# Three edits around TensorE's longest waits: a scan in four pieces, the last block's squares summed by matmul, the last output group channel by channel

## The chip, the cores and the metric

The kernel runs on one core of one Trainium2 chip. The metric is the device time of one execution in microseconds; lower is better. Engines are named as the profile names them: PE (TensorE matmul; PEld its weight loads), DVE (VectorE), ACT (ScalarE), POOL (GpSimd), SP (SyncE, which issues most DMAs). All data are 32-bit floating point. A matmul of type fp32r takes one pass; one of plain fp32 shows as two passes in the profile.

## The reference

One encoder layer on 2048 prompt tokens and, with the same weights, on 256 sample tokens (2304 in all), model width 1024:

```python
def encoder_layer(x, ...):
    h = rmsnorm(x, norm1_w)
    p = h @ w_in
    mq, mk, mv, mo, gates, aq, ak, av = jnp.split(p, cuts, axis=-1)
    m_out = mlstm_mixer(mq, mk, mv, mo, gates, b_gates, mh_norm_w)   # both directions, 8 heads of 64
    a_out = attention_mixer(aq, ak, av, q_norm_w, k_norm_w)          # 8 query heads, 2 key heads, rotary
    x = x + jnp.concatenate([m_out, a_out], axis=-1) @ w_out
    h = rmsnorm(x, norm2_w)
    u = centred_dwconv(h @ w_up, conv_w, conv_b)                     # width 3
    a, g = jnp.split(u, 2, axis=-1)
    return x + (jax.nn.silu(g) * a) @ w_down                         # inner width 2816
y = rmsnorm(encoder_layer(x, ...), final_norm_w)
# rmsnorm(x, w): x * rsqrt(mean(x * x) + 1e-6) * w
# mLSTM, per step: m_new = max(logf + m, i)  (the running maximum that stabilises the gates, forward and backward)
```

## The kernel before, in words

Tokens lie along the free axis in most stages (channels on the 128 partitions), in 18 tiles of 128 tokens. Products at full precision are made of three fp32r products each, of high and low halves (`split`, `split_w`: ACT rounds the high half, DVE subtracts to get the low half). The stages, in order of time:

- `phase_a` (0 to about 180 us): per tile the attention projections and gate pre-activations, `post1` (rotary) and `post2`; after each four tiles `gates(i0, n)` computes log-sigmoids and, tile by tile, PE transposes them and ACT (L307) copies them into `g.rows` (40 partitions, 2 rows, 2304 tokens): row 0 the input gate, row 1 the forget gate; partitions 0 to 7 are the forward heads, 32 to 39 the backward heads.
- `gate_math` (about 180 to 235 us): for both sequences (`SEGS`) a forward scan along tokens (L363) and a backward scan (L365) on DVE, state = max(state + logf, i). PE then transposes the scanned rows (L401, tiles `gpt`) for the exponents of the mLSTM.
- Attention and mLSTM, interleaved, with the output projection (`phase_c`, L983) in their later part (to about 1830 us). PE's mLSTM projections (L711, tiles `mj`; L721, tiles `mv`) share one PSUM buffer, which ACT empties (L717, L724, L727). `phase_c` takes blocks of 256 tokens in `ORDER`, the last of them block 7: four groups `z` of two channels; `post` adds the residual (L990), squares on ACT (L993) and sums on DVE into `acc` (L995); `tail` folds `acc` (L998), calls `rstd_bc` and scales (L1002). The last block's `tail` is `c_end`, called when the first two column groups of the feed-forward have begun.
- `phase_d`: `up_phase` (to about 2817 us; products L1140, a one-level Strassen-like scheme with seven products; input splits L1064 and L1065, weight splits L1112 and L1113, weight sums L1098), then `down_phase` (products L1399), three blocks of 768 tokens in two halves, each half's output in two groups of four channels. `add` adds a PSUM bank to the accumulator (L1387) and at the last product of a half calls `square`: ACT squares (L1353), POOL adds the squares up (L1357) except in the very last group (`end`), where each square is kept by itself, and ACT scales by the final norm's weight (L1358). `finish` calls `rstd_bc`, multiplies (L1365) and stores (L1366).

`rstd_bc` gives 1/sqrt(mean of squares + EPS), on all partitions: per 128 tokens PE multiplies each square tile with a column of ones (L128), DVE adds EPS (L131), then POOL raises to -1/2 (L142) or, with `act`, ACT takes the root (L135) and DVE inverts it and refines it once (L136 to L140); PE broadcasts the result to all partitions (L144).

What sets the order: the tile framework writes each engine's instruction sequence at build time from a planned timeline (`schedule_with_timeline_sim=True`), with priorities that follow the program's order; `tc.high_priority(offset=...)` moves some ahead (the splits of the feed-forward's late inputs among them). On the chip each engine works its sequence in that order, and semaphores hold an instruction until its inputs are there.

Of the kernel before, what the change touches and what calls it, by code (L numbers as in the profile page):

```python
# [119 lines left out]
def rstd_bc(g, sp, pp, sqs, n, ptag, name, bufs=1, act=False):  # L120


    nc = g.nc
    k = n // P
    ps = pp.tile([P, 512], F32, tag=ptag, name="rs_" + name, bufs=bufs)
    for t in range(k):
        for i, sq in enumerate(sqs):
            nc.tensor.matmul(ps[:, 504 + 2 * t:506 + 2 * t], sq[:, t * P:(t + 1) * P], g.ones, start=i == 0,  # L128
                             stop=i == len(sqs) - 1)
    r = sp.tile([P, 4], F32, tag="rcol", name="rcol_" + name)[:, 0:k]  # L130
    nc.vector.tensor_scalar(r, ps[:, 504:504 + 2 * k].rearrange("p (t o) -> p t o", o=2)[:, :, 0], EPS, None, ALU.add)  # L131
    if act:
        v = r
        r, u = (sp.tile([P, 4], F32, tag=f"rcol{z}", name=f"rcol{z}_" + name, bufs=1)[:, 0:k] for z in range(2))
        nc.scalar.activation(r, v, AF.Sqrt)  # L135
        nc.vector.reciprocal(r, r)  # L136
        nc.vector.tensor_tensor(u, r, r, ALU.mult)
        nc.vector.tensor_tensor(u, u, v, ALU.mult)
        nc.vector.tensor_scalar(u, u, -0.5, 1.5, ALU.mult, ALU.add)
        nc.vector.tensor_tensor(r, r, u, ALU.mult)  # L140
    else:
        nc.gpsimd.tensor_tensor(r, r, g.mhalf[:, 0:k], ALU.pow)  # L142
    for t in range(k):
        nc.tensor.matmul(ps[:, t * P:(t + 1) * P], r[:, t:t + 1].to_broadcast([P, P]), g.ident, start=True, stop=True)  # L144
    return ps[:, 0:n]


def phase_a(g, tc, sw, st_x, after_x, after_mm, after_pj):
# [3 lines left out]
    with ExitStack() as st:  # L152
# [132 lines left out]
        def gates(i0, n):  # L285

            f = g.gtm[:, i0:i0 + n, 1, :]
            t4 = sp.tile([P, 4, 4, 16], F32, tag="t4", name=f"t4_{i0}", bufs=1)
            na, u, ln, dl = (t4[:, k, 0:n] for k in range(4))
            nc.vector.scalar_tensor_tensor(na, f, -1.0, f, ALU.mult, ALU.min)  # L290
            nc.scalar.activation(na, na, AF.Exp)
            nc.vector.tensor_scalar(u, na, 1.0, None, ALU.add)
            nc.vector.scalar_tensor_tensor(dl, u, 1.0, na, ALU.subtract, ALU.subtract)
            nc.scalar.activation(ln, u, AF.Ln)
            nc.scalar.activation(g.lnr[:, i0:i0 + n], g.rt[:, i0:i0 + n], AF.Ln)
            nc.vector.tensor_scalar(u, u, -0.5, 1.5, ALU.mult, ALU.add)
            nc.vector.tensor_tensor(dl, dl, u, ALU.mult)
            nc.vector.tensor_tensor(ln, ln, dl, ALU.subtract)
            nc.vector.scalar_tensor_tensor(f, f, 0.0, ln, ALU.min, ALU.subtract)
            for i in range(i0, i0 + n):  # L300
                gp = gps[i % 3]
                nc.vector.tensor_copy(gp.rearrange("p a (b z) -> p a b z", b=2)[:, :, :, 0:8],
                                      g.gtm[:, i].rearrange("p a (b h) -> p a b h", b=2))
                pg = pp.tile([40, 2, P], F32, tag="pk", name=f"pg{i}")
                for a in range(2):
                    nc.tensor.transpose(pg[:, a, :], gp[:, a, 0:40], g.ident)
                nc.scalar.activation(g.rows[:, :, i * P:(i + 1) * P], pg, AF.Copy)  # L307

        def post2(i, kz):
            pk = pp.tile([P, 2, P], F32R, tag="pk", name=f"pk{i}")  # L310
# [45 lines left out]
def gate_math(g, tc):  # L356
# [3 lines left out]
    m = frow  # L360
    for (c0, c1) in SEGS:
        s = slice(c0 * P, c1 * P)
        nc.vector.tensor_tensor_scan(m[0:8, s], frow[0:8, s], irow[0:8, s], 0.0, ALU.add, ALU.max)  # L363
        r = slice(c1 * P - 1, c0 * P - 1 if c0 else None, -1)
        nc.vector.tensor_tensor_scan(m[32:40, r], frow[32:40, r], irow[32:40, r], 0.0, ALU.add, ALU.max)  # L365
    with ExitStack() as st:
# [572 lines left out]
def phase_c(g, sn, sp, pp, wps):  # L939
# [49 lines left out]
    def post(b, z, x, po, acc):  # L989
        nc.vector.tensor_tensor(x[z], po, x[z], ALU.add)  # L990
        g.st.dma_start(g.x1_d[b, :, 2 * z:2 * z + 2], x[z])
        q = acc if z == 0 else sp.tile([P, 2, BT], F32, tag="sq", name=f"csq{b}_{z}", bufs=1)
        nc.scalar.activation(q, x[z], AF.Square, scale=1.0 / 32.0)  # L993
        if z:
            nc.vector.tensor_tensor(acc, acc, q, ALU.add)  # L995

    def tail(b, x, acc):
        nc.vector.tensor_tensor(acc[:, 0], acc[:, 0], acc[:, 1], ALU.add)  # L998
        r = rstd_bc(g, sp, pp, [acc[:, 0]], BT, "r", f"c{b}", act=b == ORDER[-1])
        for z in range(4):  # L1000
            for o in range(2):
                nc.vector.scalar_tensor_tensor(x[z][:, o], x[z][:, o], g.n2w[:, 2 * z + o:2 * z + o + 1],  # L1002
                                               r, ALU.mult, ALU.mult)
            (nc.gpsimd if b == ORDER[-1] else g.st).dma_start(g.n2_d[:, 2 * z:2 * z + 2, b * BT:(b + 1) * BT], x[z])
        g.normed.add(b)
# [309 lines left out]
def down_phase(g, tc, st, s1, sl, banks):  # L1315
# [33 lines left out]
    def square(accs, b, c, z, sms, end):  # L1349
        a = accs[c][:, Z[z]]  # L1350
        first = not sms
        q = sp.tile([P, H], F32, tag=f"sm{z}" if first else "sq", name=f"sq{b}_{c}_{z}", bufs=1 if first else SQB)
        nc.scalar.activation(q, a, AF.Square, scale=1.0 / 32.0)  # L1353
        if first or end:
            sms.append(q)
        else:
            nc.gpsimd.tensor_tensor(sms[0], sms[0], q, ALU.add)  # L1357
        nc.scalar.activation(a, a, AF.Copy, scale=g.fw[:, c:c + 1])  # L1358

    def finish(accs, b, z, sms, bank):  # L1360
        r = rstd_bc(g, sp, bank, sms, H, "p", f"d{b}_{z}", bufs=4)

        def out(c):
            a = accs[c][:, Z[z]]
            nc.vector.tensor_tensor(a, a, r, ALU.mult)  # L1365
            g.st.dma_start(g.yT[c, :, b * BLK + z * H:b * BLK + (z + 1) * H], a)  # L1366
        for c in range(NCC):
            out(c)
# [3 lines left out]
    for b in range(ND):  # L1372
# [18 lines left out]
        def mul(ps, k, more):  # L1391
            for g0, g1 in ((0, 4), (4, 8), (8, NG)):
                t = act_tile(b, k, g0, g1)
                for z in range(g0, g1, 2):
                    for i, w in enumerate(wts(b, k, z, min(z + 2, g1))):
                        gi = z + i
                        for c in range(HALF):
                            for m, (aa, bb) in enumerate(((0, 0), (0, 1), (1, 0))):
                                nc.tensor.matmul(ps[c], w[:, aa, c, :], t[:, gi - g0, bb, 0:H],  # L1399
                                                 start=gi == 0 and m == 0 and not more,  # L1400
                                                 stop=gi == NG - 1 and m == 2, skip_group_check=more)
        p1 = newbanks(one, "f")
        mul(p1, "11", False)
        add(p1, 0, 0, False)
# [18 lines left out]
def body(tc, aps, phases="abcd"):  # L1423
# [5 lines left out]
    with ExitStack() as st:  # L1429
# [24 lines left out]
        nc.vector.tensor_copy(g.identr, g.ident)  # L1454
        g.mhalf = kp.tile([P, 16], F32, name="mhalf")
        nc.gpsimd.memset(g.mhalf, -0.5)
        g.ones = kp.tile([P, 2], F32, name="ones")
        nc.gpsimd.memset(g.ones, 1.0)
        nw = kp.tile([P, 3, NCC], F32, name="nw")
# [172 lines left out]
```

## Time and profile before

| | |
|---|---|
| median of 3 runs | 3344.66 us (3342.89 to 3348.4) |
| the profiled execution's own time | 3337.43 us |
| its span, first to last instruction | 3335.7 us |
| instructions | 53337 |
| PE busy | 3248.2 us |
| DVE, ACT, POOL busy | 2429.6, 2003.1, 512.4 us |
| mean granted TensorE clock | 0.988 |

How to read the profile's rows. A timeline row has start, duration, engine, source line, operation, output and input by name, shapes, count, and in brackets the idle time of that engine just before it with what ended it. Several instructions of one line in a row are merged into one row with their count. A row of waits reads "who waited <- for what: us in total, times, longest". A row of stretches has the stretch, its length, then busy time and instruction count of PE, PEld, DVE, ACT and POOL, the granted clock, the busy share of the DMA engines and GB/s. Names are cut to their stem: `rs_c` is the PSUM tile of `rstd_bc` for `phase_c`, `rs_d` that for `down_phase`; `rcol` their small columns; `cacc`, `csq` and `cx` the sums, squares and residuals of `phase_c`.

### The profile page before, as it was taken

How to read it: one execution, taken by the hardware profiler on the slowest of the kernel's cores; microseconds unless marked ns; L12 is line 12 of the kernel's file. 1: busy time of each engine (PE TensorE's matmuls, PEld its weight loads, DVE VectorE, ACT ScalarE, POOL GpSimd, SP SyncE). 2: the span in 40 equal slices, each digit the busy share in tenths (PEclk: the TensorE clock that was granted, in tenths of full speed). 3: DMA queues.
4: the chain of work that ended last, by engine and by line, in shares of the span. 5: the costliest groups of instructions: out<-in, count | busy, mean ns of one | idle time of the engine just before them, and what ended most of it. 6: DMA issues, size and time to landing. Idle time of an engine off the chain costs nothing.

```text
span 3335.7 us, 53337 instructions
## 1 busy us (share of the span) xinstructions
PE 3248.2 (97%) x19494; PEld 3025.2 (91%) x19494; DVE 2429.6 (73%) x3765; ACT 2003.1 (60%) x3769; POOL 512.4 (15%) x915
## 2 busy tenths in 40 slices
PE   8989999999999999999999899999999999999998
PEld 7878888888887878878889899999999999999998
DVE  7755676677657777776665999998888788656664
ACT  5646666666665676665552555666676667454543
POOL 4551033213232322300000000000000000020201
PEclk9999999999999999999999899999999999999999
DMA  9973333333335433533227666668576567967663
GB/s 354 315 202 108 112 113 102 110 110 92 109 113 176 128 113 116 169 97 106 85 88 269 227 237 213 232 231 274 204 262 240 193 211 243 321 222 274 223 237 112
DMA packets 364301, 612.31 MB, mean 184 GB/s; under 512 B 31605, under 2 KB 220455, under 8 KB 364039
## 3 DMA queue, kind: packets, MB, share of 16 engines
q1 hardware_dynamic: 330727, 563.14, 50.1%
q0 software_dynamic: 11856, 33.96, 3.7%
q10 hardware_dynamic: 21456, 11.80, 1.2%
q8 instruction: 154, 2.52, 0.3%
q14 instruction: 108, 0.88, 0.1%
HBM read 444.85 MB, written 163.93 MB: 183 GB/s over the span
## 4 chain that ended last, share of the span: by engine, by line
PE 77%; issue 6%; DMA 5%; DVE 5%; ACT 4%; POOL 2%; SPq 0%; POOLq 0%; ACTq 0%; DVEq 0%
PE pa L1140 17%; PE pc L1140 8%; PE pf L1399 5%; PE po L983 5%; PE pj L237 5%; PE pb L1140 4%; PE mj L711 4%; PE mv L721 3%; PE ps L576 3%; PE ps L577 3%; PE pv L593 3%; PE pv L595 3%; PE pv L594 3%; PE px L553 2%; PE ph L1399 2%
## 5 line engine op out<-in xcount | busy, mean ns | idle before, releaser
L582 DVE TENSOR_TENSOR xx<-pe,xx 128x1024 fp32r<-128x1024 f32 x260 | 319.1, 1228 | 127.3 <-ACT xx L581 125.8
L555 DVE TENSOR_REDUCE mx<-px 128x1 f32<-128x1024 f32 x256 | 311.0, 1218 | 101.3 <-PE px L553 100.1
L580 ACT ACTIVATE pe<-ps 128x1024 f32<-128x1024 f32 x260 | 266.3, 1024 | 172.5 <-PE ps L577 163.4
L581 ACT ACTIVATE xx<-pe 128x1024 fp32r<-128x1024 f32 x260 | 274.9, 1058 | 5.2 <-ACT pe L580 0.3
L1357 POOL TENSOR_TENSOR sq<-sq,sq 128x384 f32<-128x384 f32 x38 | 49.3, 1296 | 1377.5 <-ACT sq L1353 1296.4
L983 PEld LDWEIGHTS po<-cmx,wo 128*128 128x128 f32 x1728 | 227.3, 189 | 16.7 <-ACT wo L105 0.8
L1144 ACT ACTIVATE u<-pa 128x386 f32<-128x386 f32 (+2 forms) x264 | 129.0, 489 | 177.6 <-PE pa L1140 171.5
L983 PE MATMUL po<-cmx,wo 128*128 128x256 f32 x1728 | 234.3, 282 | 0.5 <-ACT wo L105 0.2
L593 PE MATMUL pv<-xx,vv 128*128 128x512 f32 x520 | 212.1, 408 | 6.6 <-ACT xx L581 3.9
L595 PE MATMUL pv<-xx,vv 128*128 128x512 f32 x520 | 211.0, 406 | 7.1 <-DVE xx L582 7.0
L576 PE MATMUL ps<-qq,kk 128*128 128x512 f32 x520 | 214.4, 412 | 3.4 <-ACT pe L580 2.8
L577 PE MATMUL ps<-qm,kl 65*128 65x512 f32 x520 | 209.3, 403 | 0.0
L594 PE MATMUL pv<-xx,vl 128*64 128x512 f32 x520 | 207.0, 398 | 0.0
L711 PEld LDWEIGHTS mj<-mn,wm 128*128 128x128 f32 x1296 | 177.8, 192 | 16.9 <-ACT og L727 3.2
L711 PE MATMUL mj<-mn,wm 128*128 128x256 f32 x1296 | 190.6, 287 | 2.1 <-ACT og L727 2.1
L721 PE MATMUL mv<-wm,mn 128*128 128x256 f32 x1296 | 188.4, 286 | 1.5 <-ACT qb L717 1.5
L721 PEld LDWEIGHTS mv<-wm,mn 128*128 128x128 f32 x1296 | 174.6, 190 | 14.1 <-ACT qb L717 2.5
L237 PE MATMUL pj<-w_a,n1T 128*128 128x512 f32 (+1 forms) x864 | 167.8, 353 | 9.7 <-ACT w_a L105 7.0
L553 PE MATMUL px<-kk,qq 128*128 128x512 f32 x512 | 166.5, 406 | 3.3 <-ACT pe L580 3.1
L237 PEld LDWEIGHTS pj<-w_a,n1T 128*128 128x128 f32 x864 | 141.2, 192 | 29.5 <-ACT w_a L105 7.0
L822 ACT ACTIVATE dm<-dm,tm 128x128 f32<-128x128 f32 x288 | 95.6, 392 | 97.9 <-POOL dm L819 97.4
L1140 PE MATMUL pc<-nt,wb 128*128 128x386 f32 (+2 forms) x792 | 147.5, 340 | 0.1
(331 smaller groups left out, 8123.4 us busy)
## 6 DMA issues: line engine op xcount, KB each, us to landing
mn<-n_d SPq DMA_DIRECT2D x216, 256.0 KB, 3.2
ru<-w_up SPq DMA_DIRECT2D x88, 512.0 KB, 5.6
rs<-wsu_d SPq DMA_DIRECT2D x88, 512.0 KB, 5.4
act_d<-ts SPq DMA_DIRECT2D x33, 768.0 KB, 5.2
nt<-act_d SPq DMA_DIRECT2D x60, 384.0 KB, 5.0
re_t<-wsd_d SPq DMA_DIRECT2D x45, 512.0 KB, 5.2
wsu_d<-tw SPq DMA_DIRECT2D x44, 512.0 KB, 4.0
act_d<-ya SPq DMA_DIRECT2D x99, 192.0 KB, 2.2
```

Source lines behind the costliest of these rows:

```text
L237: nc.tensor.matmul(pjs[t][:, c0:c1], nTs[tiles[t]][:, c, a, :], ws[c][:, b, c0:c1], start=(c == 0 and k == 0), stop=(c == NCC - 1 and k == 2))
L555: nc.vector.tensor_reduce(s.mx[:, t0, z0:z0 + 1], ps, AX.X, ALU.max)
L576: nc.tensor.matmul(o, kk[:, kc:kc + P], s.qq, start=True, stop=False)
L577: nc.tensor.matmul(o, kl1[:, kc:kc + P], s.qm, start=False, stop=True)
L582: nc.vector.tensor_tensor(x[:, 1], pe, f32(x[:, 0]), ALU.subtract)
L593: nc.tensor.matmul(s.pv, vv[:, kt % 4, :], x1, start=kt == 0, stop=False)
L594: nc.tensor.matmul(s.pv[0:HD], vl[:, kt % 4, :], x1, start=False, stop=False)
L595: nc.tensor.matmul(s.pv, vv[:, kt % 4, :], x2, start=False, stop=kt == s.nk - 1)
L711: nc.tensor.matmul(pj[:, o].rearrange("p (n t) -> p n t", t=P), s.w[c][:, a, o * P:(o + 1) * P], nT[c][:, :, h, :], start=(c + o + k == 0) ...
L721: nc.tensor.matmul(pv[:, o], nT[c][:, o, a, :], s.w[c][:, h, 256:512], start=(c + o + k == 0), stop=(c == NCC - 1 and k == 2 and o == 1))
L983: nc.tensor.matmul(po[:, o], wo[c][z // 2][:, a, n], mx[c][:, h, :], start=c + o + k == 0, stop=c == NCC - 1 and o == 1 and k == 2)
L1140: s.nc.tensor.matmul(p, w[:, aa, c, :], ops[k][:, c, bb, 0:s.n], start=c == 0 and i == 0 and not add, stop=c == NCC // 2 - 1 and i == 2, s ...
```

## The change

- The forward scan of the long sequence leaves `gate_math`. `gates` runs it in four pieces of 512 tokens, each as soon as its four tiles are in `g.rows`, each starting from the last column of the piece before. The backward scan and the short sequence's scans stay.
- In `phase_c`'s last block the square of the last group isn't added on DVE; PE sums four square tiles (two of `acc`, two of the last group) by accumulating the products with ones in PSUM.
- In `rstd_bc` with `act` (that block alone) ACT takes the root of the sum in PSUM directly, EPS being its bias (a constant column `g.eps`, one more memset at the start); the EPS sum on DVE stays for the refinement, which is written in one DVE instruction less.
- In `down_phase` the last product group of the last half is issued channel by channel instead of row by row; for all groups both weight splits are emitted ahead of the group's matmuls. Three of the last four squares are summed into the first by DVE, one stays by itself. The last four channels aren't scaled by ACT; their output is made in one scalar_tensor_tensor, value times weight times root.

```diff
@@ rstd_bc
+    if act:
+        sr = sp.tile([P, 4], F32, tag="rcol0", name="rcol0_" + name, bufs=1)[:, 0:k]
+        nc.scalar.activation(sr, ps[:, 504:504 + 2 * k].rearrange("p (t o) -> p t o", o=2)[:, :, 0], AF.Sqrt, bias=g.eps)
     nc.vector.tensor_scalar(r, ps[:, 504:504 + 2 * k].rearrange("p (t o) -> p t o", o=2)[:, :, 0], EPS, None, ALU.add)
     if act:
-        v = r
-        r, u = (sp.tile([P, 4], F32, tag=f"rcol{z}", name=f"rcol{z}_" + name, bufs=1)[:, 0:k] for z in range(2))
-        nc.scalar.activation(r, v, AF.Sqrt)
+        v, r = r, sr
+        u = sp.tile([P, 4], F32, tag="rcol1", name="rcol1_" + name, bufs=1)[:, 0:k]
         nc.vector.reciprocal(r, r)
-        nc.vector.tensor_tensor(u, r, r, ALU.mult)
+        nc.vector.scalar_tensor_tensor(u, r, -0.5, r, ALU.mult, ALU.mult)
         nc.vector.tensor_tensor(u, u, v, ALU.mult)
-        nc.vector.tensor_scalar(u, u, -0.5, 1.5, ALU.mult, ALU.add)
-        nc.vector.tensor_tensor(r, r, u, ALU.mult)
+        nc.vector.scalar_tensor_tensor(r, u, 1.5, r, ALU.add, ALU.mult)
@@ phase_a, gates (behind the loop that fills g.rows)
+            if i0 < NT1:
+                c, e = slice(i0 * P, (i0 + n) * P), i0 * P - 1
+                nc.vector.tensor_tensor_scan(g.rows[0:8, 1, c], g.rows[0:8, 1, c], g.rows[0:8, 0, c],
+                                             g.rows[0:8, 1, e:e + 1] if i0 else 0.0, ALU.add, ALU.max)
@@ gate_math
-        nc.vector.tensor_tensor_scan(m[0:8, s], frow[0:8, s], irow[0:8, s], 0.0, ALU.add, ALU.max)
+        if c0:
+            nc.vector.tensor_tensor_scan(m[0:8, s], frow[0:8, s], irow[0:8, s], 0.0, ALU.add, ALU.max)
@@ phase_c, post
-        if z:
+        if z == 3 and b == ORDER[-1]:
+            g.last_sq = q
+        elif z:
             nc.vector.tensor_tensor(acc, acc, q, ALU.add)
@@ phase_c, tail
-        nc.vector.tensor_tensor(acc[:, 0], acc[:, 0], acc[:, 1], ALU.add)
-        r = rstd_bc(g, sp, pp, [acc[:, 0]], BT, "r", f"c{b}", act=b == ORDER[-1])
+        if b == ORDER[-1]:
+            sqs = [acc[:, 0], acc[:, 1], g.last_sq[:, 0], g.last_sq[:, 1]]
+        else:
+            nc.vector.tensor_tensor(acc[:, 0], acc[:, 0], acc[:, 1], ALU.add)
+            sqs = [acc[:, 0]]
+        r = rstd_bc(g, sp, pp, sqs, BT, "r", f"c{b}", act=b == ORDER[-1])
@@ down_phase, square
-        if first or end:
+        if first or end and c == NCC - 1:
             sms.append(q)
         else:
-            nc.gpsimd.tensor_tensor(sms[0], sms[0], q, ALU.add)
-        nc.scalar.activation(a, a, AF.Copy, scale=g.fw[:, c:c + 1])
+            (nc.vector if end else nc.gpsimd).tensor_tensor(sms[0], sms[0], q, ALU.add)
+        if not end:
+            nc.scalar.activation(a, a, AF.Copy, scale=g.fw[:, c:c + 1])
@@ down_phase, finish, out
-            nc.vector.tensor_tensor(a, a, r, ALU.mult)
+            if (b, z) == (ND - 1, 0) and c >= HALF:
+                nc.vector.scalar_tensor_tensor(a, a, g.fw[:, c:c + 1], r, ALU.mult, ALU.mult)
+            else:
+                nc.vector.tensor_tensor(a, a, r, ALU.mult)
@@ down_phase, mul
-                for z in range(g0, g1, 2):
-                    for i, w in enumerate(wts(b, k, z, min(z + 2, g1))):
-                        gi = z + i
-                        for c in range(HALF):
-                            ...
+                ws = [(z, wts(b, k, z, min(z + 2, g1))) for z in range(g0, g1, 2)]
+                steps = [(z + i, w[i], c) for z, w in ws for i in range(len(w)) for c in range(HALF)]
+                if (b, k, g1) == (ND - 1, "t4", NG):
+                    steps.sort(key=lambda v: v[2])
+                for gi, w, c in steps:
+                    ...
```

More of the change, by code (lines that the diff above doesn't have):

```diff
@@ L1456, in body @@
         nc.gpsimd.memset(g.mhalf, -0.5)
+        g.eps = kp.tile([P, 1], F32, name="eps")
+        nc.gpsimd.memset(g.eps, EPS)
         g.ones = kp.tile([P, 2], F32, name="ones")
```

8 lines of the change are left out of this document (4 added, 4 removed).

## The prediction, written before the change was run

> **What bounds the kernel now.** The page's first part comes first: which engine has no room. Then the table of stretches shows where that engine has room after all, and the waits name what ends it.
>
> ```profile
> span 3335.7 us, 53337 instructions
> ...
> PE 3248.2 (97%) x19494; PEld 3025.2 (91%) x19494; DVE 2429.6 (73%) x3765; ACT 2003.1 (60%) x3769; POOL 512.4 (15%) x915
> ```
>
> ```profile
> core 0: us, PE busy (x) PEld busy (x) DVE busy (x) ACT busy (x) POOL busy (x), PEclk, DMA share, GB/s
> 10.00:170.00 160.00, 157.69 (x870) 137.56 (x870) 127.52 (x301) 93.94 (x175) 80.68 (x104) 0.99 1.00 335
> 210.00:1440.00 1230.00, 1196.05 (x7464) 1039.10 (x7463) 834.08 (x1552) 803.80 (x1817) 338.26 (x682) 0.99 0.40 122
> 1829.90:1849.80 19.90, 1.92 (x10) 1.82 (x9) 18.76 (x29) 12.13 (x15) 0.00 (x0) 0.56 0.94 334
> 1880.00:2817.00 937.00, 937.00 (x5333) 936.85 (x5332) 822.35 (x1008) 607.97 (x1058) 0.00 (x0) 1.00 0.66 229
> 3318.30:3335.70 17.40, 7.41 (x35) 6.86 (x34) 4.50 (x11) 2.94 (x7) 0.85 (x1) 0.56 0.25 90
> ```
>
> ```profile
> PE rs_c L144 <- DVE rcol_c L140: 10.3, 1, 10.3
> PE rs_c L128 <- DVE cacc L998: 7.7, 1, 7.7
> ...
> PE gpt L401 <- DVE rows L365: 3.3, 1, 3.3
> ```
>
> TensorE is the bound: 87.5 us of a 3335.7 us span are not PE's. In the up stage (1880 to 2817) it has no idle time at all, so what is won ahead of it is kept. The idle time sits in lumps: 18.0 us at the join between output projection and feed-forward (1829.9 to 1849.8, where DVE is busy 18.76 of 19.90 us), 3.3 us behind the gate scans, and the end after the last product. These are the three places that the diff edits, and I cost each by itself. A fourth lump, 34.0 us thinly spread over 210 to 1440, isn't edited and comes back as a rival.
>
> **The scan in pieces.**
>
> ```profile
> 65.51 0.68 DVE L363 TENSOR_TENSOR_SCAN rows<-rows 8x256 f32<-8x256 f32 x1 [2.00 <-ACT rows L307]
> ...
> 192.15 4.41 DVE L363 TENSOR_TENSOR_SCAN rows<-rows 8x2048 f32<-8x2048 f32 x1 [0.48 <-ACT rows L307]
> 196.58 4.41 DVE L365 TENSOR_TENSOR_SCAN rows<-rows 8x2048 f32<-8x2048 f32 x1
> ```
>
> ```profile
> 194.12 3.58 PE L721 MATMUL mv<-wm,mn 128*128 128x256 f32 x28
> 201.05 0.86 PE L401 MATMUL gpt<-ident,rows 40*128 40x40 f32 x6 [3.34 <-DVE rows L365]
> ...
> 203.04 1.22 PE L711 MATMUL mj<-mn,wm 128*128 128x256 f32 x4
> ```
>
> Two points give the scan's price: (4.41 - 0.68) / (2048 - 256) = 2.08 ns a column and 0.15 us fixed, so a 512-column piece costs 1.21 us. Only the fourth piece stays behind the last rows: 1.21 + 4.41 instead of 8.82 us, and the backward scan ends at 197.8 instead of 201.0. PE's stalled transposes wait behind L721, which ends at 197.70, so the 3.34 us wait nearly goes. What is late next: L711 needs the bank that ACT's last read gives back.
>
> ```profile
> 199.67 0.62 ACT L727 ACTIVATE og<-mv,rh 128x128 f32<-128x128 f32 x2
> ```
>
> That ends at 200.29, so L711 starts no earlier than 200.35 against 203.04: at most 2.7 us, and at least zero if PE's order puts L711 ahead of the transposes. I take 2.5, near the upper end, since the transposes fit between 197.8 and 200.3. The other three pieces run inside the first stage: 3 x 1.21 us of added DVE work where DVE idles 32 of 160 us. I cost them at nothing under that cover; if each delays a PE step they cost 3.6 us.
>
> **The join.** Removed on DVE: one 128x512 sum (L995), one 128x256 sum (L998) and one of five small steps in the root. L131's added constant leaves the path, because ACT takes the root from PSUM with the constant as its bias; L131 still runs. Added on PE: 12 matmul passes (four squares by two tiles by two passes, instead of 4). The constant's one memset stands among POOL's first and costs nothing.
>
> ```profile
> 1833.57 0.69 DVE L995 TENSOR_TENSOR cacc<-cacc,csq 128x512 f32<-128x512 f32 x1
> ...
> 1837.12 0.42 DVE L998 TENSOR_TENSOR cacc<-cacc 128x256 f32<-128x256 f32 x1
> ...
> 1840.07 1.22 DVE L1113 TENSOR_TENSOR wb<-tw,wb 128x1024 fp32r<-128x1024 f32 x1
> ...
> 1843.21 0.15 DVE L131 TENSOR_SCALAR rcol_c<-rs_c 128x2 f32<-128x2 f32 x1
> 1843.28 1.82 DVE L1065 TENSOR_TENSOR n<-n 128x772 fp32r<-128x772 f32 x2
> 1845.02 1.22 DVE L1113 TENSOR_TENSOR wc<-tw,wc 128x1024 fp32r<-128x1024 f32 x1
> 1846.16 1.83 DVE L1065 TENSOR_TENSOR nt<-nt 128x772 fp32r<-128x772 f32 x2
> 1847.90 0.15 DVE L136 RECIPROCAL rcol_c<-rcol_c 128x2 f32<-128x2 f32 x1
> ```
>
> ```profile
> 1830.74 0.63 ACT L993 ACTIVATE csq<-cx 128x512 f32<-128x512 f32 x1 [5.07 <-DVE cx L990]
> ...
> 1843.62 1.28 ACT L135 ACT_TABLE_LOAD   x1
> 1844.91 0.20 ACT L135 ACTIVATE rcol_c<-rcol_c 128x2 f32<-128x2 f32 x1
> ```
>
> ```profile
> 1837.59 1.01 PE L128 MATMUL rs_c<-ones,cacc 128*128 128x2 f32 x4 [7.68 <-DVE cacc L998]
> 1848.91 1.22 PE L144 MATMUL rs_c<-ident,rcol_c 128*128 128x128 f32 x4 [10.30 <-DVE rcol_c L140]
> ```
>
> The last square is ready at 1831.37, but its sum waits in DVE's queue: L995 starts 2.2 us later, L998 a further 3.6 us, and L131 runs 4.6 us after PE has delivered. With the change, 14 passes (two of 16 can go ahead) at 0.25 us follow the square directly, and PE delivers at 1834.9 instead of 1838.6. Three bounds for what follows:
> - Least: the last DVE steps stay behind the same queue of splits (L1065, L1113). Then only the removed DVE work counts, 0.69 + 0.42 + 0.2 = 1.3 us; zero if ACT's earlier root delays the splits behind it by its 1.48 us.
> - Most: root at once, 1834.9 + 1.5 = 1836.4; four DVE steps of 0.2 us with a split of 1.22 us between each, 1840.9; against 1848.9, where PE is released, that is 8.0 us. PE's next products need the second wb split, which ends at 1841.29, so they could start about then.
> - Taken: the root goes between ACT's splits near 1838 and ends at 1839.5. DVE's first step then falls behind one or two splits more (1842), and its four steps with a split between each reach 1846.5, 0.9 us less for removed work: 1845.6, against 1848.9: 3.3 us.
>
> I stay nearer the lower end because in the row before it DVE ran 4.9 us of splits between L131 and L136, although the root needed 1.6. DVE has 18.76 us of work there whatever the order. The eight scalings of L1002 follow the chain and move with it; PE's next products don't read them.
>
> [...]
>
> **The end.**
>
> ```profile
> 3311.74 6.50 PE L1399 MATMUL pf<-nt,we_t 128*128 128x384 f32 x36
> 3318.07 0.75 PE L128 MATMUL rs_d<-ones,sq 128*128 128x2 f32 x6
> ...
> 3320.28 4.85 PE L128 MATMUL rs_d<-ones,sq 128*128 128x2 f32 x22 [0.53 <-ACT sq L1353]
> ```
>
> ```profile
> 3319.72 0.51 ACT L1353 ACTIVATE sq<-acc 128x384 f32<-128x384 f32 x1
> ```
>
> ```profile
> 3318.30:3319.30 1.00, 0.53 (x5) 0.44 (x4) 0.53 (x2) 1.00 (x4) 0.00 (x0) 1.00 0.00 0
> 3320.20:3321.20 1.00, 0.92 (x5) 0.92 (x5) 0.00 (x0) 1.00 (x3) 0.00 (x0) 0.56 0.00 0
> ```
>
> Before, four channels finish three products (3 x 6.50 / 36 = 0.54 us) apart, ACT squares and scales them alternately, and the last square ends at 3320.23; 22 passes then take 4.85 us, to 3325.13. Afterwards each channel takes nine products, 1.62 us, so three of four are added, squared and summed on DVE (0.55, 0.51 and 0.55 us) before the last is out at 3318.24. The scalings leave ACT. The last square ends near 3319.5, one 0.1 us being lost to DVE's sum; two sources instead of five leave 10 passes behind it. At the slow rate (4.85 / 22 = 0.22 us) they end at 3321.7, at the fast one (0.75 / 6 = 0.125) at 3320.75: a gain of 3.4 to 4.4 us. Against it four outputs become scalar_tensor_tensor.
>
> ```profile
> L1365 DVE TENSOR_TENSOR acc<-acc,rs_d x48: 545/548/555, 2974.4 to 3331.3; 128x384 f32<-128x384 f32 x48
> ```
>
> ```profile
> L1002 DVE SCALAR_TENSOR_TENSOR cx<-cx,nw,rs_c x72: 472/476/482, 1524.3 to 1852.9; 128x256 f32<-128x256 f32 x72
> ```
>
> At 1.05 ns a column (L995 against L998) the plain product of L1365 would take 0.41 us at 256 columns, where L1002 takes 0.476: 0.06 us more each, 0.24 us for four. I take 3.1, the slow rate less that. The sort needs all weights of the last group at its start.
>
> ```profile
> 3299.05 1.23 DVE L1113 TENSOR_TENSOR we_t<-re_t,we_t 128x1024 fp32r<-128x1024 f32 x1 [3.73 <-ACT we_t L1112]
> ```
>
> The last split ends at 3300.28, 11 us ahead, so the sort costs nothing; without that cover it costs one split, 1.23 us. Emitting both splits of a group ahead of its products changes no engine's own sequence, since between them only PE has work.
>
> The clock decides between the two rates. In the rows it is full to 3319.3 and 0.56 from 3320.2, some two us behind the last dense product. [...]
>
> **Sum.** 2.5 + 3.3 + 3.1 = 8.9 us. The profiled execution took 3337.43 us (span 3335.7 and 1.7 around it) and would take 3328.5. The median of the runs shown is 3344.66, 7.2 above that execution, so the forecast is 3344.7 - 8.9 = 3335.8. A difference of 0.2%, 6.7 us, is about what can be told from no change.
>
> **The rivals.**
> - The root's chain stays at the back of DVE's queue: 2.5 + 1.3 + 3.1 = 6.9, 3337.8 us. For it: DVE is 94% busy there. Against it: the chain is ready 3.7 us sooner.
> - The chain goes early: 2.5 + 8.0 + 3.1 = 13.6, 3331.1 us. For it: ACT is busy only 12.13 of 19.90 us. Against it: the 4.9 us between L131 and L136.
> - The scan moves nothing, because L711 or another product takes the place of the wait: 3.3 + 3.1 = 6.4, 3338.3 us. For it: L711 is free at 200.35, among the transposes. Against it: then L711 itself runs in the time that PE now waits, which is the gain by another road.
> - Slower: the build writes each engine's order from planned times, and shorter scans shift the plan of all that follows. The place is the mix of attention and recurrence, 210 to 1440, with 34.0 us of PE idle in many small waits. If a new order makes that half as much again, +17.0 - 8.9 = +8.1, 3352.8 us; it decides from 8.9 + 6.7 = 15.6 us of new idle. For it: that stretch's DVE and ACT are 68% and 65% busy and any order of theirs makes waits. Against it: all its work shifts by the same 2.5 us, which changes little of who is ready first.
>
> **How the numbers follow.** Forecast 0.50 (its own range 3332 to 3339), chain at the back 0.20, chain early 0.13, scan without effect 0.09, new order 0.08. Faster by over 0.2%: 0.41 of the forecast, half of the second, all of the third, a little under half of the fourth, 0.67; slower is the last with 0.01 of the others, 0.09; the rest, 0.24, lies within. The range leaves out half of the new order and some at the low end: the low end is all upper bounds (2.7 + 8.0 + 4.1 = 14.8, 3329.9) less 3 us for a plan that falls better; the high end is the lower bounds (0 + 0 + 3.1, 3341.6) with 3.6 us for the scan's pieces on the path.
>
> **What would show it.** Four 8x512 scans, three before 170 us; PE's wait for L365 under 0.5 us; no L995 for the last square, 16 passes in L128 and the wait at L144 cut to about 7 us; 10 passes behind the last square and the last scaling about 3 us sooner after the last product. The forecast is wrong if PE's idle time in 210 to 1440 moves by over 5 us, or if the join's splits are waited for instead of the root.

## The result, and the profile after

The changed kernel takes 3332.66 us (median of 6 runs, 3324.33 to 3335.36) against 3342.5 us for the kernel before beside it (3338.93 to 3348.4): a ratio of 0.9964, 95% interval 0.995 to 0.9978, so 9.8 us less by the medians and 7 to 17 us less by the interval. The 3332.66 us lie at the low edge of the forecast's own range, 3332 to 3339. Timed a second time (e10 below) it was 0.9971 (0.9961 to 0.9982), again 9.9 us by the medians. The profiled execution took 3327.39 us, with a span of 3325.7 us against 3335.7 before.

The head of the page after, then the table of stretches (the join from the last output product to the first up product, the up stage, and the end behind the last down product, each at its place in this execution):

```profile
span 3325.7 us, 53327 instructions
...
PE 3238.2 (97%) x19488; PEld 3017.3 (91%) x19488; DVE 2429.5 (73%) x3768; ACT 2002.8 (60%) x3765; POOL 519.0 (16%) x916
```

```profile
core 0: us, PE busy (x) PEld busy (x) DVE busy (x) ACT busy (x) POOL busy (x), PEclk, DMA share, GB/s
210.00:1440.00 1230.00, 1194.82 (x7482) 1038.34 (x7481) 837.22 (x1564) 809.42 (x1827) 341.96 (x685) 0.99 0.40 122
1825.60:1844.80 19.20, 2.81 (x22) 2.63 (x20) 17.46 (x26) 11.96 (x15) 0.00 (x0) 0.62 0.97 339
1880.00:2817.00 937.00, 937.00 (x5336) 936.85 (x5335) 822.11 (x1008) 608.94 (x1062) 0.00 (x0) 1.00 0.67 231
3313.30:3325.70 12.40, 2.43 (x18) 2.16 (x18) 5.23 (x11) 0.52 (x1) 0.85 (x1) 0.70 0.35 127
```

PE's busy time fell by 10.0 us, as the span did, and its idle time stayed at 87.5 us. Some 4 us of that are the end's fewer and faster passes (4.85 to 1.50 us, and the broadcast 1.65 to 0.93); another execution of the changed kernel (e10) has 3242.9 us of busy PE, so most of the rest lies within what executions of one kernel differ by. PE's waits at the edited places:

```profile
PE rs_c L145 <- DVE rcol_c L141: 15.2, 1, 15.2
...
PE mj L717 <- ACT og L733: 2.9, 4, 1.0
...
PE rs_c L128 <- ACT csq L999: 1.2, 1, 1.2
...
PE gpt L407 <- DVE rows L371: 0.2, 1, 0.2
```

The gate scans are no longer waited for (3.3 us before). At the join the wait for the squares fell from 7.7 to 1.2 us, and the wait for the root grew from 10.3 to 15.2. Between the two profiles, four landmarks divide the 10.0 us of span: up to the first product behind the scans 1.5 us; from there to the last output product 2.8 us; the join 19.87 to 19.11, 0.8 us; the up and down stages -0.1; the end 17.42 to 12.35, 5.1 us.

### The profile page after: what moved, and what is told of

Its sections match the earlier page's. It is cut to its first block, busy times and chain, and to the rows that moved or that the text cites. A ratio compares the mean times of both kernels' runs of the same rounds, so it can differ in the third digit from the quotient of the medians.

```text
span 3325.7 us, 53327 instructions
## 1 busy us (share of the span) xinstructions
PE 3238.2 (97%) x19488; PEld 3017.3 (91%) x19488; DVE 2429.5 (73%) x3768; ACT 2002.8 (60%) x3765; POOL 519.0 (16%) x916
## 4 chain that ended last, share of the span: by engine, by line
PE 58%; issue 3%; DVE 2%; DMA 2%; ACT 2%; POOL 1%; SPq 0%; POOLq 0%; DVEq 0%; ACTq 0%
PE pa L1152 17%; PE pc L1152 8%; PE pf L1416 7%; PE po L989 5%; PE pb L1152 4%; PE ph L1416 4%; PE pg L1416 2%; PE ps L582 1%; PE mj L745 1%; PE ps L583 1%; PE pv L599 1%; PE pv L601 1%; PE pv L600 1%; PE px L559 1%; PE mv L745 1%
## 5 line engine op out<-in xcount | busy, mean ns | idle before, releaser
L1369 POOL TENSOR_TENSOR sq<-sq,sq 128x384 f32<-128x384 f32 x38 | 48.8, 1284 | 1377.9 <-ACT sq L1365 1294.9
```

## The experiments

In all of them the stretches are read from one profiled execution each, so I first need to know how much one sequence of instructions moves by itself.

**e1, the kernel before, once more (no edit).** It was run in the first group beside e2, e3 and e4.

> The kernel before, unchanged, profiled a second time. Both kernels have the same sequence of instructions on every engine between 210 and 1800 us, yet the profile after was 2.8 us shorter there. If that is the spread of single executions, this profile will differ from the first one of before by 2 to 5 us in the same stretch, with the join (last output-projection product to first product of the next stage, 19.9 us) and the end (start of the last product group to the end of the span, 24.0 us) the same to 0.3 us. If instead the change caused it, this stretch agrees with the first profile to 0.5 us.

One run of 3341.24 us, span 3339.5. The stretch from the scans to the output projection took 1631.84 us instead of 1626.87, the join 19.86, and the end 15.18 instead of 17.42. Its end, in the order of time (PE):

```profile
3326.32 2.62 PE L128 MATMUL rs_d<-ones,sq 128*128 128x2 f32 x22 [0.53 <-ACT sq L1353]
...
3330.19 1.65 PE L144 MATMUL rs_d<-ident,rcol_d 128*128 128x128 f32 x6 [1.25 <-POOL rcol_d L142]
```

The same 22 passes that took 4.85 us in the first profile take 2.62 us here: the granted clock stayed at 1.00 to 4.8 us behind the last dense product and was 0.50 from there on. So 5 us in the middle and 2.2 us at the end separate two executions of one program: the spread that I expected in the middle is there, and the end, which I expected to repeat to 0.3 us, does not.

**e2, the scan in pieces alone** (the kernel before with this part of the change):

```diff
+            if i0 < NT1:
+                c, e = slice(i0 * P, (i0 + n) * P), i0 * P - 1
+                nc.vector.tensor_tensor_scan(g.rows[0:8, 1, c], ...)
...
+        if c0:
+            nc.vector.tensor_tensor_scan(m[0:8, s], ...)
```

> Before with the scan in four pieces alone. If the parts act each in its own place: the first product behind the scans (tile mj) starts 2.0 to 2.7 us sooner, measured from the end of the product ahead of it (tile mv) to mj: 3.9 us instead of 5.4; PE's wait for the backward scan under 0.5 instead of 3.3 us; the three earlier pieces cost less than 1 us in the first stage; the whole 1.5 to 2.5 us faster, ratio near 0.9994; join and end as in before (19.9 and 24.0 us). If the shifted plan mattered, the whole would move by over 4 us either way.

3337.54 us against 3339.57, ratio 0.9994 (0.9984 to 1.0005). From the end of the last attention product ahead of the scans to the first product behind them PE needs 2.64 us instead of 5.33, but the stretch behind it took 1633.45 us in this execution. (The 5.33 is not a constant either: in e1 the products just ahead ended at 200.13 us and not at 197.70, and the same distance was 3.64 us.) The local gain is there; the whole can't tell 2 us from nothing.

**e3, the join alone** (root from PSUM, the last squares summed by PE):

```diff
+        sqs = [acc[:, 0], acc[:, 1], g.last_sq[:, 0], g.last_sq[:, 1]]
...
+        nc.scalar.activation(sr, ps[:, 504:504 + 2 * k]..., AF.Sqrt, bias=g.eps)
...
```

> Before with the join's edits alone (squares summed by PE, root from the sum in PSUM). Theory 1, the chain's four DVE steps fall apart between the splits in DVE's queue: from the last product of the output projection to the first of the next stage 19.1 instead of 19.9 us, PE's wait for the root's result about 15 instead of 10.3 us, the whole 0.8 us faster, not to be told from no change. Theory 2, as forecast (chain done some three us sooner): 16.6 us, the whole 3.3 us faster, ratio 0.9990.

3336.97 us, ratio 0.999 (0.998 to 0.9999). The join is 19.02 us instead of 19.87, with 15.1 us of wait for the root's last step: 0.85 us, as theory 1 had it and not the 16.6 of the forecast.

**e4, the end alone** (sums on DVE, two sources, scaling in one product, last group by channel):

```diff
+        if first or end and c == NCC - 1:
...
+            (nc.vector if end else nc.gpsimd).tensor_tensor(sms[0], sms[0], q, ALU.add)
...
+                if (b, k, g1) == (ND - 1, "t4", NG):
+                    steps.sort(key=lambda v: v[2])
```

> Before with the end's edits alone. If the clock stays full through all passes behind the last square: start of the last product group to the end of the span 18.9 instead of 24.0 us, twelve passes in 1.5 us, the whole 5.1 us faster, ratio 0.9985. If the slow rate of before held, as forecast: 20.9 us, 10 to 12 passes in 2.2 to 2.6 us, the whole 3.1 us faster, ratio 0.9991. Everything up to the last group as in before.

3336.64 us, ratio 0.9988 (0.9979 to 0.9996); the end is 12.36 us with 12 passes in 1.50 us, the case of the full clock (granted 1.00 to 4.8 us behind the last dense product), and join and scan are as before.

**e10, the changed kernel once more (no edit)**, beside e9.

> The changed kernel once more, timed beside the run before it on the same chip. By all theories its instruction sequence is that of the changed kernel: the stretch from the scans to the output projection's last product should differ from the 1624.0 us of its first profile by what executions of one sequence differ by (the kernel before: 1626.9 and 1631.8), the join be 19.1 us, the end 12.35 us if TensorE's clock stays full through the broadcast and 13.2 us if it falls ahead of it (as in e5 and e6), and its time 8 to 11 us below the kernel before.

3331.43 us against 3341.31, ratio 0.9971 (0.9961 to 0.9982). Join 19.11, end 12.36, and 1628.22 us in the middle instead of 1624.03. So the first two profiles' difference of 2.8 us there is within what executions of one kernel differ by. Over all 14 executions, the four with the long scan spent 1626.6 to 1631.8 us in the middle (mean 1628.9), the ten with the pieces 1623.9 to 1633.5 (mean 1628.0).

**e7, all five sources of squares kept at the end** (in the changed kernel):

```diff
-        if first or end and c == NCC - 1:
+        if first or end:
...
-            (nc.vector if end else nc.gpsimd).tensor_tensor(sms[0], sms[0], q, ALU.add)
+            nc.gpsimd.tensor_tensor(sms[0], sms[0], q, ALU.add)
```

> The changed kernel's end with all five sources of squares kept for PE, as before the change, instead of two (no sums of squares on DVE; 40 passes instead of 16). The end (last down product to the end of the span) took 12.35 us in the changed kernel and 15.2 to 17.4 us in executions of the kernel before. If TensorE's clock falls about two us after the last dense product, as the prediction had it, 22 or so passes behind the last square run partly at 0.22 us and the end is about 15 us. If it stays full for as long as the changed kernel's broadcast showed (about 4 us after the last dense product), the passes take 22 x 0.125 = 2.75 us in place of 1.50, less the 0.6 us that DVE's last sum costs PE: the end is 13.0 us if the broadcast is still fast, 13.7 if it runs at the slow rate (1.65 in place of 0.93).

```profile
3316.16 2.62 PE L128 MATMUL rs_d<-ones,sq 128*128 128x2 f32 x22 [0.48 <-ACT sq L1365]
...
3320.02 1.65 PE L145 MATMUL rs_d<-ident,rcol_d 128*128 128x128 f32 x6 [1.25 <-POOL rcol_d L143]
```

The end is 14.41 us, 2.06 more than in the changed kernel. The granted clock stayed at 1.00 for 4.5 us behind the last dense product, through the passes, and was 0.50 under the broadcast: 1.12 us more of passes and 0.72 of broadcast. My 13.7 us counted on 0.6 us back from DVE's last sum. That was wrong: the passes start 1.27 us behind the last product here and 1.11 us in the changed kernel, where DVE's last sum (3313.81 to 3314.36) runs beside ACT's last square (3313.99 to 3314.51) and so costs PE nothing.

**e8, the last group's products not ordered by channel** (in the changed kernel):

```diff
-                if (b, k, g1) == (ND - 1, "t4", NG):
-                    steps.sort(key=lambda v: v[2])
```

> The changed kernel without the ordering of the last group's products by channel: the four channels finish three products (0.54 us) apart again, while the sums of squares on DVE, the two sources and the scaling in one product stay. By the prediction's steps three of the four channels are then added, squared and summed later than the last product: DVE has up to four additions of 0.55 us and three sums of 0.4 us in a row behind it, so the end is 1 to 2.7 us longer than 12.35 us (13.4 to 15). If the ordering does nothing because ACT or the store chain sets the end, it stays at 12.4 us.

```profile
3313.35 2.37 PE L128 MATMUL rs_d<-ones,sq 128*128 128x2 f32 x12 [2.19 <-DVE sq L1369]
```

15.01 us, at the upper end of what was expected. The passes start 2.19 us behind the last product instead of 1.11. The granted clock fell from 1.00 to 0.50 2.6 us behind it, so the same 12 passes took 2.37 us instead of 1.50 and the broadcast 1.65 instead of 0.93. Of the 2.66 us that this end is longer, the order's part is the later start, 1.1 us; the other 1.6 us are this execution's earlier fall of the clock.

**e5, the root by POOL's power, and the last group's scalings written to another tile** (in the changed kernel):

```diff
-        r = rstd_bc(g, sp, pp, sqs, BT, "r", f"c{b}", act=b == ORDER[-1])
+        r = rstd_bc(g, sp, pp, sqs, BT, "r", f"c{b}", act=False)
...
+            y = acc if z == 3 and b == ORDER[-1] else x[z]
...
```

> The changed kernel, with the last block's root taken by POOL's power (one DVE step to PSUM's sums, then POOL, then PE; instead of ACT's root and four DVE steps), and the last group's eight scalings written into acc, so that none of them waits for the store of x1. In the changed kernel the join (end of the last output product to the first up product) took 19.11 us, and each of the four DVE steps stood behind a split in DVE's queue. Theory A, the chain's length in steps of DVE's queue is what holds PE: with one DVE step the broadcast leaves PE's wait of 15.2 us at 6 us or less, and the join falls to 8 to 10 us, unless the second bank of the up stage, which the scalings give back, is waited for next; the whole 5 to 9 us faster than the changed kernel. Theory B, PE's next product waits for the splits and DVE's total work of about 18.8 us there whatever the chain does: the broadcast comes early, but the idle time moves to the first up products (waits for a split or a bank of 10 us and more in sum), and the whole gains 2 us or less.

```profile
PE rs_c L145 <- POOL rcol_c L143: 7.2, 1, 7.2
PE pa L1153 <- ACT u L1157: 5.9, 1, 5.9
```

```profile
1855.42 0.88 ACT L1157 ACTIVATE u<-pa 128x386 f32<-128x386 f32 x2 [9.93 <-DMA n_d<-cacc]
```

The join fell to 11.10 us, and 5.9 us came back 13 us later: ACT's copy out of PSUM waited for the store of the tile that I had chosen, and PE for ACT. 3333.01 us, ratio 0.9971 (0.9961 to 0.9981): no better than the changed kernel. Theory A had the direction of the first wait right (15.2 to 7.2 us, where it said 6 or less, and a join of 8 to 10), and no eye for this one. Theory B's sum, a gain of 2 us or less, came true, but what PE waited for was a store and not the splits.

**e6, the same without the other tile.**

```diff
+        r = rstd_bc(g, sp, pp, sqs, BT, "r", f"c{b}", act=False)
```

> As the run before it, without the edit to acc: the root by POOL's power alone, so the last of the eight scalings still waits for the store of x1 and stands behind two more splits in DVE's queue. Theory A (steps in DVE's queue): the broadcast comes as early as in the run before, the first up product starts about 9 us sooner than in the changed kernel (join 8 to 10 us), but the second bank comes back only with the last scaling, so that the idle time up to the second up group shrinks by about 4 us; the whole 2 to 5 us faster than the changed kernel. Theory B (splits and total DVE work): the same as the changed kernel within 2 us.

```profile
1830.46 1.22 PE L145 MATMUL rs_c<-ident,rcol_c 128*128 128x128 f32 x4 [2.88 <-POOL rcol_c L143]
...
1842.38 3.79 PE L1152 MATMUL pc<-nt,wb 128*128 128x386 f32 x12 [5.66 <-DVE cx L1014]
```

The last scaling and what stands ahead of it in DVE's queue:

```profile
1834.13 2.43 DVE L1014 SCALAR_TENSOR_TENSOR cx<-cx,nw,rs_c 128x256 f32<-128x256 f32 x6
1836.48 1.83 DVE L1077 TENSOR_TENSOR nt<-nt 128x772 fp32r<-128x772 f32 x2
...
1840.23 1.22 DVE L1125 TENSOR_TENSOR wc<-tw,wc 128x1024 fp32r<-128x1024 f32 x1
1841.37 0.86 DVE L1014 SCALAR_TENSOR_TENSOR cx<-cx,nw,rs_c 128x256 f32<-128x256 f32 x2
```

The join is 6.75 us. The second up group starts 17.8 us behind the last output product (22.9 in the changed kernel), held by the last scaling, which stands behind five splits. 3329.22 us, ratio 0.9963 (0.995 to 0.9976): as a whole not to be told from the changed kernel (0.9964 and 0.9971). With one DVE step in place of four, the broadcast came 12.4 us sooner after the same products: theory B's bound by DVE's total work falls for the first group; the second still waits for a step behind splits.

**e9, e6 with the last group's store of x1 issued by POOL.** The last scaling overwrites the store's source, so it must come after the store. On the chip it was not the store that held it in e6: the three stores of this line that SP issued between 1815 and 1856 us took 3.1 us to land by the median, and DVE worked without a gap from 1824.62 to the scaling at 1841.37. So what the edit can change is the place that the build gives the scaling in DVE's queue.

```diff
-        g.st.dma_start(g.x1_d[b, :, 2 * z:2 * z + 2], x[z])
+        (nc.gpsimd if z == 3 and b == ORDER[-1] else g.st).dma_start(g.x1_d[...], x[z])
```

> The changed kernel with the root by POOL's power (as in e6) and the last group's store of x1 issued by POOL instead of SP, where it stood behind loads that wait. In e6 the first up product came 12.4 us sooner, but 5.7 us of it went back at the second up group, whose bank waits for the last scaling (1841.37 to 1842.2), and that scaling stood behind the store of its own input. Theory A (the chain's place in DVE's queue and the release of that bank are all that holds PE here): join 6 to 7.5 us, the wait at the second group 2.5 us or less instead of 5.7, the up and down stages up to the last down product 1470 to 1472 us instead of 1474.9, and the whole 8 to 11 us faster than the changed kernel, about 3320 against a kernel before at 3340. Rival: DVE's 15 or so splits in this place are what PE needs in the end, so the idle time moves on to the next split (a wait for wb, wc or n of 4 us and more), and the whole gains the 6 us of e6 and no more.

Four rows in the order of time, from POOL, DVE and PE:

```profile
1831.07 5.70 POOL L143 TENSOR_TENSOR rcol_c<-rcol_c,mhalf 128x2 f32<-128x2 f32 x1 [0.21 <-DVE rcol_c L134]
...
1833.84 2.35 DVE L1125 TENSOR_TENSOR wb<-tw,wb 128x1024 fp32r<-128x1024 f32 x2
...
1836.83 1.22 PE L145 MATMUL rs_c<-ident,rcol_c 128*128 128x128 f32 x4 [7.25 <-POOL rcol_c L143]
...
1842.33 2.34 PE L1152 MATMUL pc<-nt,wb 128*128 128x386 f32 x12 [1.14 <-DVE cx L1014]
```

3322.23 us against 3341.31, ratio 0.9942 (0.993 to 0.9954), where the changed kernel on the same chip had 0.9971 (0.9961 to 0.9982): 9.2 us faster than the changed kernel, with intervals that don't meet. The second group now starts 15.8 us behind the last output product, 7.1 sooner. In DVE's queue one split (1840.83) stands between the last scaling and the seven others, where five stood ahead of the last two in e6. The wait at the second group is 1.14 us (2.5 or less expected). The join itself, 11.13 us, missed the 6 to 7.5 expected: POOL's power lasted 5.70 us. The up and down stages took 1464.8 us, below the 1470 to 1472 expected, and that part isn't explained by the edit.

**e11, the root on ACT with the reciprocal alone on DVE** (e9's store; no POOL in the chain; DVE's added constant and the Newton correction of the last block's root left out):

```diff
-        v, r = r, sr
...
+        r = sr
         nc.vector.reciprocal(r, r)
-        nc.vector.scalar_tensor_tensor(u, r, -0.5, r, ALU.mult, ALU.mult)
-        nc.vector.tensor_tensor(u, u, v, ALU.mult)
-        nc.vector.scalar_tensor_tensor(r, u, 1.5, r, ALU.add, ALU.mult)
```

> The changed kernel with the last group's store of x1 issued by POOL (as in e9), ACT's root from PSUM kept, and only its reciprocal left on DVE: the added constant and the three steps of the Newton correction behind it are left out for the last block. In e9 POOL's power of 128x2 elements took 5.70 us (0.72 in the other blocks) while DVE ran eight splits and sums without a gap, and it ended 0.6 us after they did; in e6 it took 1.34 us in the same place. Theory C, POOL is held up by DVE's two-input instructions in a row: without POOL in the chain the root costs 1.28 us of table load and 0.26, the reciprocal runs behind one sum or split, and the broadcast comes 6 to 7 us after the last output product instead of 10.3, in every execution; the second up group then starts when DVE has done its 8 scalings, about 14 us after the last output product (15.8 in e9, 17.8 in e6, 22.9 in the changed kernel), and the whole is 1 to 2.5 us faster than e9. Rival: the chain's own length (the table load, the semaphores) keeps the broadcast at 9 us or later, and the time is e9's within 0.5 us.

```profile
1839.59 1.22 PE L141 MATMUL rs_c<-ident,rcol_c 128*128 128x128 f32 x4 [2.81 <-DVE rcol_c L136]
...
1848.09 3.04 PE L1148 MATMUL pc<-nt,wb 128*128 128x386 f32 x12 [1.77 <-DVE cx L1010]
```

The broadcast comes 6.2 us behind the last output product (1833.37) and the second group 14.7 us, the figures that theory C gave (6 to 7 and about 14). That is 1 us sooner than in e9, and the time does not show it: 3323.11 us, ratio 0.9939 (0.9925 to 0.9952), against e12's 0.9935.

**e12, e9's kernel once more (no edit)**, beside e11.

> e9's kernel once more, beside e11 on the same chip. Theory C: POOL's power falls again either at 1.3 us (it starts before DVE's next two-input instruction) or at 5.7 us (it starts behind it), and the broadcast stands at about 6 or 10.3 us behind the last output product accordingly. The whole again 8 to 10 us below the changed kernel's place, that is 17 to 20 us below the kernel before.

3320.55 us against 3343.47, ratio 0.9935 (0.9921 to 0.9949). POOL's power took 5.70 us again and the broadcast stood at 10.25 us, the second of the two cases expected. That is 22.9 us below the kernel before by the medians, where 17 to 20 were expected. Of the versions that leave nothing out this is the fastest, and it beats both the kernel before and the changed one.

## Why the prediction came out as it did

The forecast was 3335.8 us with 8.9 us of gain, and the measured gain is 9.8. Of its three terms two had the right size and one was too large, and something that it did not have made up for that: the closeness of the total is in part luck.

**The scan (2.5 forecast) was right.** In the trace after:

```profile
193.38 1.27 DVE L311 TENSOR_TENSOR_SCAN rows<-rows 8x512 f32<-8x512 f32 x1 [0.49 <-ACT rows L308]
194.67 4.41 DVE L371 TENSOR_TENSOR_SCAN rows<-rows 8x2048 f32<-8x2048 f32 x1
...
200.90 0.63 ACT L733 ACTIVATE og<-mv,rh 128x128 f32<-128x128 f32 x2
...
201.58 2.72 PE L717 MATMUL mj<-mn,wm 128*128 128x256 f32 x12 [0.97 <-ACT og L733]
```

The piece takes 1.27 us (1.21 worked out), and what is late next is the product that waits for ACT's last read, as forecast. The first product stands 2.64 us behind the last one ahead of the scans, where it stood 5.33. Over the executions it starts at 203.0 to 204.4 us with one long scan (four, mean 203.8) and at 200.7 to 202.9 with the pieces (ten, mean 201.5): 2.3 us. The three early pieces cost nothing that shows.

**The join (3.3 forecast) was mis-sized; it gave 0.8.** The failing step is the one headed "Taken". It was right that the chain starts sooner: PE delivers the sums 3.0 us behind the last output product instead of 8.7 (5.0 forecast: the 12 passes behind the square took 1.50 us, 0.125 each and not 0.25), and ACT the root 5.8 us behind it instead of 15.2. It was wrong in what DVE then does:

```profile
1829.85 1.28 ACT L133 ACT_TABLE_LOAD   x1
1831.15 0.26 ACT L133 ACTIVATE rcol_c<-rs_c,eps 128x2 f32<-128x2 f32 x1
```

```profile
1831.59 0.15 DVE L138 RECIPROCAL rcol_c<-rcol_c 128x2 f32<-128x2 f32 x1
...
1833.72 1.22 DVE L1125 TENSOR_TENSOR wb<-tw,wb 128x1024 fp32r<-128x1024 f32 x1
1834.86 0.15 DVE L139 SCALAR_TENSOR_TENSOR rcol_c<-rcol_c 128x2 f32<-128x2 f32 x1
...
1837.81 1.22 DVE L1125 TENSOR_TENSOR wc<-tw,wc 128x1024 fp32r<-128x1024 f32 x1
1838.95 0.15 DVE L140 TENSOR_TENSOR rcol_c<-rcol_c,rcol_c 128x2 f32<-128x2 f32 x1
...
1841.90 1.82 DVE L1077 TENSOR_TENSOR nt<-nt 128x772 fp32r<-128x772 f32 x2
1843.64 0.15 DVE L141 SCALAR_TENSOR_TENSOR rcol_c<-rcol_c,rcol_c 128x2 f32<-128x2 f32 x1
```

The root is there at 1831.41 and the reciprocal runs at 1831.59, 12 us sooner in its stretch than before. (ACT's root starts 0.02 us behind the end of the table load's 1.28 us here, and 0.01 us in the trace before.) But the three steps after it stand four or five sums and splits apart, 3.3, 4.1 and 4.7 us, not one split of 1.22 us. PE's wait for the root, forecast to fall from 10.3 to about 7 us, rose to 15.2. The last one ends 18.2 us behind the last output product, where it ended 18.9 before. So the rival "the chain stays at the back of DVE's queue" is what happened, and its sum of 6.9 us for the whole is near what the three places gave (below). Here, the queue's order was the cost and not a lack of room: e6 and e11, with one DVE step behind the sums, broadcast 6 us after the last product, with DVE's other work unchanged. What spoke against that rival, that "the chain is ready 3.7 us sooner", was true (5.7 us even) and of no use.

**The end (3.1 forecast) gave 5.1 between the two profiles, and 2.8 to 3.7 at equal clocks.** PE's two rows and the outputs after:

```profile
3314.41 1.50 PE L128 MATMUL rs_d<-ones,sq 128*128 128x2 f32 x12 [1.11 <-DVE sq L1369]
...
3317.09 0.93 PE L145 MATMUL rs_d<-ident,rcol_d 128*128 128x128 f32 x6 [1.18 <-POOL rcol_d L143]
3318.07 1.95 DVE L1381 TENSOR_TENSOR acc<-acc,rs_d 128x384 f32<-128x384 f32 x4 [1.95 <-PE rs_d L145]
3319.93 2.18 DVE L1379 SCALAR_TENSOR_TENSOR acc<-acc,nw,rs_d 128x384 f32<-128x384 f32 x4
```

The steps held: three channels are done early, the outputs cost 0.23 us more (0.24 forecast), and 12 passes run behind the last product, the first of them 0.1 us before the last square is out (10 behind that square were forecast). What differs is the rate: 0.125 us each, not 0.22, and the broadcast at the full clock too, 0.93 us instead of 1.65. I took the clock's fall "some two us behind the last dense product" for a property of the kernel. Placing the fall by half-microsecond slices of the granted clock, which is 1.00 ahead of it and 0.50 behind it, the 14 executions have it 2.0 to 5.3 us behind the last dense product, and the end's length follows it (the columns take in the experiments that have the one end or the other):

| fall behind the last dense product, us | end of the kernel before | end of the changed kernel |
|---|---|---|
| 2.0 to 2.1 | 17.42, 17.41, 17.42 | 13.71 |
| 2.7 to 3.6 | | 13.22, 13.22 |
| 4.7 to 5.3 | 15.18 | 12.35, 12.36, 12.36, 12.43, 12.57 |

At equal clocks the change is worth 3.7 us (early fall) or 2.8 (late fall), so the term's size was right and its clock was not. The means of the columns, 16.86 and 12.78, are 4.1 us apart, since three of four old ends met an early fall and one of eight new ones; whether that is chance or the change's doing, so few executions don't say. The distance is not one number even for one kernel: the falls spread over 3.2 us in the eight executions that share the changed end, and e9 and e12, one kernel, fell 2.0 and 4.7 us behind. What sets the moment no run shows. The 4.1 us in the low end of the forecast's range, old passes at 0.22 us and new ones at 0.125, less 0.24 for the outputs, no run shows by itself: equal clocks gave 2.8 to 3.7, and the two profiles, old end slow and new end fast, gave 5.1, the broadcast's 0.72 us among it.

**The rest.** 2.3 + 0.8 + 3.2 (the middle of 2.8 and 3.7) is 6.3 us, or 7.2 with the end's means. Both lie inside the second timing's interval (6.0 to 13.0 us) and below the first's (7.4 to 16.7), and they are 2.6 to 3.5 us short of the medians. That remainder stays open. The three parts timed alone (e2, e3, e4) gained 2.0, 2.6 and 2.9 us by the medians, 7.6 in sum, so no interplay of the three has to be assumed. The stretch between scans and output projection moves by 4 to 5 us between two executions of one kernel. The up and down stages took 1465.0 to 1472.4 us where no experiment's own wait is in them, and there a wait is seen to move: PE's for POOL's sums of squares in `down_phase` (L1357 before, L1369 after), 3.7 to 6.3 us in the five executions without the whole change and 1.6 to 4.5 in the nine with it. But the two plain executions of each kernel don't differ there (3.7 and 4.7 before, 4.5 and 4.2 after), and these are too few to say whether a part of the remainder belongs to the change. The rival of a new order that makes PE idle between 210 and 1440 is out: that idle time is 35.2 us after and 34.0 before. So the total came out right partly because the remainder is about as large as the 2.5 us that the join did not give.

## What to carry to other kernels

Where a short chain of small steps shares an engine with long independent work, count the places that it takes in the queue and not its busy time: taking four DVE steps down to one moved the broadcast by 8 to 12 us, where having its input 5.7 us earlier moved it by 0.8. Then follow the tiles and banks that the chain's consumers give back, since e5 and e6 gave much of the won time back at the next wait, and e9, which also moved the store and with it the last scaling's place, kept most of it. And before the clock at a kernel's end is taken as a number of the kernel, read it from more than one execution.

## What the hardware showed beside that

All powers of e9 at this place, one per block (shortest, median and longest in ns):

```profile
L143 POOL TENSOR_TENSOR rcol_c<-rcol_c,mhalf x9: 688/716/5699, 1517.0 to 1831.1; 128x2 f32<-128x2 f32 x9
```

An instruction of 0.7 us took 5.69, 5.70 and 5.70 us at the join in e5, e9 and e12, ending 0.55 to 0.58 us behind DVE's last of six sums and splits in a row. In e6 it took 1.34 us beside a row of the same six, and ended 0.55 us behind the first of them. In all four it started 0.16 to 0.18 us behind the start of that first one, so its start does not tell the short case from the long ones, though the expectation of e12 took it to do so. That POOL is held up by DVE's two-input instructions was theory C's guess: e11 shows the chain's length without POOL, and no run shows what ties the end of POOL's power to DVE's row.
